# Two mix-out blocks woven together, retention rows scaled by two heads, x by token on another queue

## The chip, the cores and the metric

The kernel runs on one core of one Trainium2 chip. The metric is the device time of one execution in microseconds (us); a lower time is better. The core has a matrix engine (TensorE, PE in the profile, with its weight loads as PEld), a vector engine (VectorE, DVE), an engine for activations and scaled copies (ScalarE, ACT), GpSimd (POOL) and SyncE (SP), whose main work here is to request transfers.

## The reference

One layer of a hybrid decoder in float32, for 256 tokens of width 2048, all weights read once from memory:

```python
hn = rmsnorm(h, norm_mix_w)
q, k, v, g_ret, xr, yr, g_a, g_b = split(hn @ w_in)
ret = head_groupnorm(chunkwise_retention(rotary(q), rotary(k) * dk**-0.5, v), ret_gn_w)
ret_out = silu(g_ret) * ret                       # 8 heads, 256 values wide
rnn_out = gelu(yr) * rg_lru(causal_dwconv(xr))
merged = sigmoid(g_a) * (ret_out @ w_proj_ret) + sigmoid(g_b) * (rnn_out @ w_proj_rnn)
h = h + merged @ w_mix_out
h = h + memory_cross_attention(rmsnorm(h), rmsnorm(mem))    # 256 memory tokens
h = h + conv_gated_ffn(rmsnorm(h))                          # 5632 wide
return rmsnorm(h, final_norm_w)
```

## The kernel before, in words

**Weights in chunks.** Every matrix product is cut into blocks of 512 output columns, and the 2048 (or more) rows of weights of a block into chunks of four times 128 rows, 1 MB each. `weight_plan` lists the blocks in order, `weight_stream` flattens them to a list of chunks; the host lays the weights out in that order, so that each chunk is one transfer. The order of the list must be the order in which the products ask for chunks. Two places of the list are woven already: the first two blocks chunk by chunk, and three of the last ones, where the last chunk of each block comes after the others.

**High and low parts.** The products keep float32's precision: a chunk lands in a tile `raw` (three buffers), ScalarE casts it to a rounded high part `hi` (L267 for the first chunk on VectorE, L269 after), VectorE subtracts to get the low part `lo` (L270), half a chunk at a time (six buffers of each). TensorE makes three products for each pair of tiles, with high and low parts of the other operand (`s`), all by `mm` at L206. In a product by tokens (`steps_n`) the 24 matmuls of a chunk run over two tiles of tokens, four row tiles and three part products. `prefetch` requests a chunk (L244) and emits its casts; it keeps two chunks ahead of the one in use.

**Steps.** `chunks` is the loop under every product: it hands out a chunk, and at each chunk's end it runs what is due. `later(n, fn)` puts `fn` off by n + 1 chunk ends. A product is a generator (`steps_n`) that `ended` runs to its end, one chunk a step.

**Turning rows.** `by_dma(rows, then, wait)` turns a block of rows by token into columns by feature: two plane copies on ScalarE (`pl`, L380, with raised priority), two transposing transfers requested by SyncE (`pt`, L382), and, `wait` + 1 chunk ends later, two copies that join the planes (`f`, L391) and a call of `then`. For merged rows `then` is `turn_merged`, which splits them in high and low parts (`split_pair`, L420 to L424); for the residual stream it is `turn` with `split_cols` (L446, L447).

**Retention heads.** The heads are done in two groups of four. A head's rows go to `rc` (L632) with their mean and variance; after the fourth head `normalise` (L644 to L653) subtracts the mean and multiplies by the gate on VectorE for four heads and two tiles of tokens, and scales each by its reciprocal deviation on ScalarE into `rows` (L653, eight instructions), then calls `by_dma` for two blocks of rows with waits 2 and 3. In the second group, the rows of the recurrent branch are already coming through the same engines: their convolution is `conv_x` (L763 on ScalarE, L765 on VectorE).

**Merge and mix-out.** `gated` makes a block of one branch's projection times its gate; four blocks `mb` of the recurrent branch, then four `m` of the retention branch, added (L820) and turned. `residual` then makes the four blocks of merged times `w_mix_out`: each block needs all four merged blocks as its other operand, one of them in each of its four chunks. After a block it adds it to the residual row block (`nat`, L835), takes squares (L850, tile `junk`) and turns it. `memory_steps` (called ahead of each block) makes at the second block the eight sums of squares of the memory's rows on ScalarE (L488) and their deviation, and at the fourth loads the memory by feature.

**Order and queues.** The program is written in program order; a scheduler orders each engine's instructions by priority and by what they depend on, and each engine then works in that fixed order. Transfers are requested on SyncE's queue; only the four blocks of x by token (tiles `nat`, `load_x`, L223) are requested by ScalarE, after the casts of the fifth to eighth chunk. Constants (`cid`, `pa`, `pb`) follow the eighth chunk's weights, `pf` the twelfth's (L250 to L254). The sums of squares of x by token (L488) are emitted with the ninth and tenth chunk.

Of the kernel before, what the change touches and what calls it, by code (L numbers as in the profile page):

```python
# [17 lines left out]
P = 128  # L18
D = 2048
S = 256  # L20
NT = D // P
HEADS = 8
DK = 128
DV = 256
# [4 lines left out]
BW = 512  # L29
KC = 4  # L30
# [76 lines left out]
    return [(sum(sizes[:j]), n) for j, n in enumerate(sizes)]  # L107


def weight_stream():  # L110

    out = [
        [(w, row + k * P, n, c) for k, n in pieces(i, nk)]
        for i, (w, row, nk, c) in enumerate(weight_plan())
    ]
    out[:2] = [[one for pair in zip(*out[:2]) for one in pair]]
    out[-4:-1] = [[c for o in out[-4:-1] for c in o[:-1]] + [o[-1] for o in out[-4:-1]]]
    return [one for chunks in out for one in chunks]


# [10 lines left out]
def hybrid_layer(  # L131
# [16 lines left out]
    act, dve, pe, pool, sp = nc.scalar, nc.vector, nc.tensor, nc.gpsimd, nc.sync  # L148
# [15 lines left out]
    def big(shape, dt=F32, s="b"):  # L164
        return bp.tile(shape, dt, tag="big", name=nm(s))
# [52 lines left out]
    def load_x(n):  # L218
        while len(xin) < n:
            t = big([P, 2, BW], s="nat")  # L220
            rows = x[0].rearrange("(t p) d -> p t d", p=P)
            c = len(xin) * BW
            act.dma_start(out=t, in_=rows[:, :, c : c + BW])  # L223
            xin.append(t)

    at = [0]
# [1 line left out]
    def prefetch(n):  # L228
        while len(ahead) < n and taken[0] < len(stream):
            i = taken[0]  # L230
            name, row, nk, c = stream[i]
            taken[0] += 1
            size = nk * P * BW
            src = wall[at[0] : at[0] + size].rearrange("(p k n) -> p k n", p=P, k=nk)
            at[0] += size
            raw = wp.tile([P, KC, BW], F32, tag="raw", bufs=RAW_BUFS, name=nm("raw"))
            k2 = row // (KH * P)
            early = i < 2 * len(EARLY)
            own = early and i % 2 == 0
            cuts = range(nk + 1) if i < 2 else range(0, nk + 1, KH) if i < 6 else (0, nk)  # L240
            if own:
                xs.load(k2 + 1)
            for a, b in zip(cuts, cuts[1:]):
                sp.dma_start(out=raw[:, a:b, :], in_=src[:, a:b, :])  # L244
                if i == 0 and a == 0:
                    sp.dma_start(out=xs.rest[0], in_=xs.rest[1])
                elif own and a == 0:
                    xs.load(k2 + nk // KH)
            if i == 7:
                sp.dma_start(out=cid, in_=consts[:, 0:C_DEC])  # L250
                sp.dma_start(out=pa[:, 16:P], in_=by_feature[:, 16:P])
                sp.dma_start(out=pb, in_=by_feature[:, P : P + 80])
            if i == 11:
                sp.dma_start(out=pf.rearrange("p a n -> p (a n)"), in_=by_feature[:, P + 80 :])  # L254
            if i in (8, 9):
                for b in (2 * i - 16, 2 * i - 15):
                    sum_squares(xin[b], ss0, b, pin=True)
            parts = []
            for k in range(0, nk, KH):
                if own:  # L260
                    xs[k2 + k // KH]
                hi = wp.tile([P, KH, BW], F32R, tag="hi", bufs=PART_BUFS, name=nm("hi"))
                lo = wp.tile([P, KH, BW], F32R, tag="lo", bufs=PART_BUFS, name=nm("lo"))
                for cs in (slice(k, k + 1), slice(k + 1, k + 2)) if i < 2 else (slice(k, k + KH),):
                    ds = slice(cs.start - k, cs.stop - k)
                    if i == 0:
                        dve.tensor_copy(hi[:, ds], raw[:, cs, :])  # L267
                    else:
                        act.copy(hi[:, ds], raw[:, cs, :])  # L269
                    dve.tensor_tensor(  # L270
                        out=lo[:, ds], in0=raw[:, cs, :], in1=hi[:, ds].bitcast(F32), op=ALU.subtract
                    )
                parts.append((hi, lo))
            ahead.append(((row, c), parts))
            if i >= 4:
                load_x(min(4, i - 3))

    pending, step = [], [0]

    def later(n, fn):  # L280

        pending.append((step[0] + n + 1, fn))
# [18 lines left out]
    def ended(steps):  # L301

        for a in steps:
            pass
        return a
# [54 lines left out]
    def gemm_n(*args):  # L360
        return ended(steps_n(*args))
# [130 lines left out]
    def sums():  # L492
        return sp_.tile([P, 2, 4], F32, tag="ss0", name=nm("ss"))
# [103 lines left out]
    ret, words = [], []  # L597
# [5 lines left out]
    def retain(g, qr, kr, vs, dec, gates):  # L603

        stats = sp_.tile([P, 8, 2], F32, tag="mv", name=nm("mv"))
        raws = []

        def scores(hh):
            sc = small((P, 384))
            k, q = kr[hh // 2], qr[hh // 2]  # L610
            product(sc[:, 0:S], halves(k, hh % 2, slice(0, P)), halves(q, hh % 2), True, True)
            late = slice(P, S)
            product(sc[:, S : S + P], halves(k, hh % 2, late), halves(q, hh % 2, late), True, True)
            pr_ = tp.tile([P, 384], F32, tag="pret", bufs=2, name=nm("pret"))
            dve.tensor_tensor(out=pr_[:, 0:S], in0=sc[:, 0:S], in1=dec[:, hh, :], op=ALU.mult)
            dve.tensor_tensor(out=pr_[:, S:384], in0=sc[:, S:384], in1=dec[:, hh, 0:P], op=ALU.mult)
            phi, plo = (tp.tile([P, 384], F32R, tag="tmp", name=nm("ps")) for _ in range(2))
            act.copy(phi, pr_)
            dve.tensor_tensor(out=plo, in0=pr_, in1=phi.bitcast(F32), op=ALU.subtract)
            later(0, lambda: values(hh, phi, plo))  # L620

        def values(hh, phi, plo):
            vc = slice((hh % 2) * DV, (hh % 2 + 1) * DV)
            v0, v1 = ([t[:, tt, vc] for t in vs[hh // 2]] for tt in range(2))
            p0, p1, p2 = ([t[:, c * P : (c + 1) * P] for t in (phi, plo)] for c in range(3))
            ro = small()
            product(ro[:, 0, :], p0, v0, True, True)
            product(ro[:, 1, :], p1, v0, True, False)
            product(ro[:, 1, :], p2, v1, False, True)
            bn = sp_.tile([P, 2, 6], F32, tag="bn", name=nm("bn"))  # L630
            rc = tmp("rc")
            act.copy(rc, ro)  # L632
            for tt in range(2):
                dve.bn_stats(out=bn[:, tt, :], in_=rc[:, tt, :])
                dve.bn_aggr(out=stats[:, 2 * hh + tt, :], in_=bn[:, tt, :])
            raws.append(rc)
            if hh == 3:
                normalise()

        def normalise():  # L640
            rows = [big([P, 2, BW], s="rows") for _ in range(2)]
            rstd = rsqrt_small(stats[:, :, 1], 8, 1.0, GN_EPS).rearrange("p (h t) -> p h t", t=2)
            for tt in range(2):
                dve.tensor_scalar_mul(rstd[:, :, tt], rstd[:, :, tt], rs0[:, tt : tt + 1])  # L644
            for hh in range(4):
                for tt in range(2):
                    y = raws[hh][:, tt, :]
                    dve.scalar_tensor_tensor(
                        out=y, in0=y, scalar=stats[:, 2 * hh + tt, 0:1],
                        in1=gates[hh // 2][:, tt, (hh % 2) * DV : (hh % 2 + 1) * DV],  # L650
                        op0=ALU.subtract, op1=ALU.mult,
                    )
                    act.mul(rows[hh // 2][:, tt, (hh % 2) * DV : (hh % 2 + 1) * DV], y, rstd[:, hh, tt : tt + 1])  # L653
            for i, r in enumerate(rows):
                by_dma(r, words.append, 2 + i)

        for hh in range(4):
            later(hh, lambda hh=hh: scores(hh))

    for g in range(2):  # L660
        dec = big([P, 4, S], s="dec")
        vs, turned = [], ([], [])
        for b, o in enumerate((O_Q, O_K)):
# [6 lines left out]
            if b == 1:  # L670
                sp.dma_start(
                    out=dec,
                    in_=consts[:, C_DEC + g * 4 * S : C_DEC + (g + 1) * 4 * S].rearrange("p (h s) -> p h s", s=S),
# [144 lines left out]
    for b in range(4):  # L818
        m = gated(O_GA, "w_proj_ret", ret, b, big([P, 2, BW], s="m"))
        dve.tensor_add(m, m, mb[b])  # L820
        by_dma(m, turn_merged)


    hrow = [load_rows(x, c) for c in range(4)]
# [3 lines left out]
    def residual(w, st, out, wcol, steps=None):  # L828

        ss = sums()  # L830
        for b in range(4):
            if steps:
                steps(b)
            h = hrow[b]
            dve.tensor_add(h, h, gemm_n(w, 0, st, NT, b * BW))  # L835
            squares(h, ss, b)
            by_dma(hrow[b], lambda f, b=b: turn(f, b, out, wcol))
        return ss
# [261 lines left out]
```

## Time and profile before

| | us |
|---|---|
| median of 3 runs | 2025.03 |
| the other two | 2021.9, 2025.69 |
| profiled execution, whole time | 2022.28 |
| its span | 2020.5 |
| TensorE busy in it | 2002.3 |
| VectorE busy | 1264.3 |
| ScalarE busy | 1246.0 |

The span is the time from the first to the last recorded instruction of the profiled execution; its whole time is 1.8 us longer. TensorE is busy for 99% of it, at a mean granted clock of 0.996 of full speed. In lines of the profile, `L206` is the helper of all matmuls, `a<-b,c` is output and inputs by tile names, and `[1.98 <-DVE lo L270]` says how long an engine stood idle ahead of the instruction and what ended that.

### The profile page before, as it was taken

How to read it: one execution, taken by the hardware profiler on the slowest of the kernel's cores; microseconds unless marked ns; L12 is line 12 of the kernel's file. 1: busy time of each engine (PE TensorE's matmuls, PEld its weight loads, DVE VectorE, ACT ScalarE, POOL GpSimd, SP SyncE). 2: the span in 40 equal slices, each digit the busy share in tenths (PEclk: the TensorE clock that was granted, in tenths of full speed). 3: DMA queues.
4: the chain of work that ended last, by engine and by line, in shares of the span. 5: the costliest groups of instructions: out<-in, count | busy, mean ns of one | idle time of the engine just before them, and what ended most of it. 6: DMA issues, size and time to landing. Idle time of an engine off the chain costs nothing.

```text
span 2020.5 us, 23630 instructions
## 1 busy us (share of the span) xinstructions
PE 2002.3 (99%) x9060; PEld 1666.2 (82%) x9060; DVE 1264.3 (63%) x1563; ACT 1246.0 (62%) x1502; POOL 7.7 (0%) x12
## 2 busy tenths in 40 slices
PE   9999999999999999999999999999999999999998
PEld 7888888888888888788888888888888888888887
DVE  5856756888645555456555554567675577664675
ACT  6546547989434555478666556666774566644763
POOL 0000000000000000000000000000000000000000
PEclk9999999999999999999999999999999999999999
DMA  8665656665555566777766546667666566655663
GB/s 304 225 210 173 234 199 192 228 213 188 208 188 190 197 204 214 259 225 242 219 198 204 182 167 208 209 189 218 228 203 232 193 195 214 227 215 198 210 228 125
DMA packets 185153, 421.99 MB, mean 209 GB/s; under 512 B 127440, under 2 KB 132176, under 8 KB 139984
## 3 DMA queue, kind: packets, MB, share of 16 engines
q1 hardware_dynamic: 183520, 417.85, 62.2%
q10 hardware_dynamic: 1520, 2.63, 0.4%
q8 instruction: 71, 1.16, 0.2%
q14 instruction: 42, 0.34, 0.1%
HBM read 388.46 MB, written 2.10 MB: 193 GB/s over the span
## 4 chain that ended last, share of the span: by engine, by line
PE 97%; ACT 1%; DVE 1%; DMA 1%; issue 1%; SPq 0%; POOL 0%; POOLq 0%; DVEq 0%; ACTq 0%
PE acc L206 94%; PE sm L206 3%; DMA raw<-in_wall 1%; DVE lo L270 0%; ACT f L391 0%; DVE xr L765 0%; ACT pl L380 0%; ACT rows L653 0%; ACT hi L269 0%; POOL ro L507 0%; PE sm L209 0%; SPq L244 0%; DVE s L447 0%; ACT nat L1034 0%; DVE rows L404 0%
## 5 line engine op out<-in xcount | busy, mean ns | idle before, releaser
L206 PE MATMUL acc<-hi,s 128*128 128x512 f32 (+1 forms) x5680 | 1741.6, 388 | 4.2 <-ACT s L423 4.0
L270 DVE TENSOR_TENSOR lo<-raw,hi 128x1024 fp32r<-128x1024 f32 (+1 forms) x714 | 861.1, 1220 | 662.4 <-ACT hi L269 636.5
L206 PEld LDWEIGHTS acc<-hi,s 128*128 128x128 f32 x5680 | 1062.5, 188 | 222.1 <-ACT s L423 4.5
L206 PE MATMUL acc<-lo,s 128*128 128x512 f32 (+1 forms) x2840 | 1100.8, 388 | 2.0 <-DVE lo L270 2.0
L269 ACT CAST hi<-raw 128x1024 fp32r<-128x1024 f32 (+1 forms) x712 | 736.0, 1051 | 535.4 <-PE acc L206 466.7
L206 PEld LDWEIGHTS acc<-lo,s 128*128 128x128 f32 x2840 | 533.7, 188 | 111.6 <-DVE lo L270 2.7
L391 ACT COPY f<-pt 128x1024 uint16<-128x1024 uint16 x114 | 146.5, 1350 | 68.8 <-DMA pt<-pl 68.6
L380 ACT COPY pl<-rows 128x1024 uint16<-128x1024 uint16 x90 | 89.8, 1046 | 66.1 <-DVE rows L404 58.2
L404 DVE TENSOR_SCALAR rows<-acc,ro 128x512 f32<-128x512 f32 x68 | 47.8, 747 | 2.4 <-PE acc L206 2.4
L957 DVE SCALAR_TENSOR_TENSOR fv<-f,pf,fv 128x255 f32<-128x255 f32 (+1 forms) x88 | 35.8, 479 | 0.7 <-ACT fv L955 0.7
L957 DVE SCALAR_TENSOR_TENSOR fg<-f,pf,fg 128x255 f32<-128x255 f32 (+1 forms) x88 | 35.6, 478 | 0.0
L955 ACT ACTIVATE fv<-f,pf 128x256 f32<-128x256 f32 x44 | 22.9, 596 | 0.0
L955 ACT ACTIVATE fg<-f,pf 128x256 f32<-128x256 f32 x44 | 22.9, 594 | 0.0
L423 ACT ACTIVATE s<-fo 128x512 fp32r<-128x512 f32 x22 | 13.6, 635 | 14.1 <-DVE fo L977 14.1
L380 ACT COPY pl<-nat 128x1024 uint16<-128x1024 uint16 x16 | 16.0, 1046 | 9.6 <-DVE nat L835 9.6
L765 DVE SCALAR_TENSOR_TENSOR xr<-f,pa,xr 128x255 f32<-128x255 f32 (+2 forms) x48 | 20.1, 481 | 2.1 <-ACT xr L763 2.0
L446 ACT ACTIVATE s<-f,pb 128x256 fp32r<-128x256 f32 x48 | 20.4, 501 | 0.0
L447 DVE SCALAR_TENSOR_TENSOR s<-f,pb,s 128x256 fp32r<-128x256 f32 x48 | 19.9, 480 | 0.0
L206 PEld LDWEIGHTS sm<-s,s 128*128 128x128 f32 x144 | 18.8, 191 | 0.9
L206 PE MATMUL acc<-s,hi 128*128 128x512 f32 x64 | 17.6, 413 | 1.0 <-DVE hi L267 1.0
L206 PE MATMUL sm<-s,s 128*128 128x256 f32 (+1 forms) x144 | 18.6, 279 | 0.0
L421 DVE TENSOR_TENSOR s<-f,s 128x512 fp32r<-128x512 f32 x16 | 10.3, 687 | 10.0 <-ACT s L420 10.0
(154 smaller groups left out, 630.0 us busy)
## 6 DMA issues: line engine op xcount, KB each, us to landing
raw<-in_wall SPq DMA_DIRECT2D x352, 1024.0 KB, 4.9
raw<-in_wall SPq DMA_DIRECT2D x6, 512.0 KB, 6.4
nat<-in_x ACTq DMA_DIRECT2D x4, 512.0 KB, 8.2
nat<-in_x SPq DMA_DIRECT2D x4, 512.0 KB, 5.7
nat<-in_mem SPq DMA_DIRECT2D x4, 512.0 KB, 9.0
xt<-in_mem_t SPq DMA_DIRECT2D x8, 256.0 KB, 3.7
pt<-pl SPq DMA_TRANSPOSE x114, 4.9
xt<-in_x_t SPq DMA_DIRECT2D x7, 256.0 KB, 6.3
```

What stands on the lines that cost most here:

```text
L206: tc.keep_in_program_order(pe.matmul(*a, **k))
L269: act.copy(hi[:, ds], raw[:, cs, :])
L270: dve.tensor_tensor(out=lo[:, ds], in0=raw[:, cs, :], in1=hi[:, ds].bitcast(F32), op=ALU.subtract)
L380: act.copy(planes[:, :, h, :], words[:, h])
L391: act.copy(halves_[:, h], turned_[:, h])
L404: dve.tensor_scalar_mul(rows[:, tt, :], a[:, tt, :], r[:, tt : tt + 1])
L423: act.mul(t[:, :, 0:S], src, scale)
L446: act.activation(t[:, j, 0:S], src[:, j, :], AF.Identity, scale=wcol(j))
L447: dve.scalar_tensor_tensor(out=t[:, j, S:BW], in0=src[:, j, :], scalar=wcol(j), in1=t[:, j, 0:S].bitcast(F32), op0=ALU.mult, op1=ALU.subtract,
L765: dve.scalar_tensor_tensor(out=y[:, s:S], in0=z[:, 0 : S - s], scalar=p_cw(3 - s, t), in1=y[:, s:S], op0=ALU.mult, op1=ALU.add,)
L955: act.activation(y, z[:, j, :], AF.Identity, scale=pf[:, 2, t : t + 1], bias=pf[:, 3, t : t + 1])
L957: dve.scalar_tensor_tensor(out=y[:, s:S], in0=z[:, j, 0 : S - s], scalar=pf[:, 2 - s, t : t + 1], in1=y[:, s:S], op0=ALU.mult, op1=ALU.add,)
```

## The change

Three places change. (1) `weight_stream` and `residual`: the first two blocks of mix-out run in turn, three chunks of the first, three of the second, then the fourth of the first and the fourth of the second (`in_turn`, which the last blocks use already in its written-out form). The last merged block is turned with a wait of 3 instead of 1. Blocks three and four stay as they were. (2) `normalise`: the scaling of rows is split into `two_heads(0)` and `two_heads(1)`, each put off by `later` to one of the next two chunk ends, each turned with a wait of 4. (3) `load_x`: x by token is requested by SyncE behind the weights of the sixth to ninth chunk; `cid`, `pa`, `pb` move behind the ninth chunk's weights, `pf` behind the fourteenth's. The number of matmuls, casts and transfers stays the same.

```diff
@@ -107,6 +107,11 @@
     return [(sum(sizes[:j]), n) for j, n in enumerate(sizes)]
 
 
+def in_turn(products):
+
+    return [c for o in products for c in o[:-1]] + [o[-1] for o in products]
+
+
 def weight_stream():
 
     out = [
@@ -114,7 +119,9 @@
         for i, (w, row, nk, c) in enumerate(weight_plan())
     ]
     out[:2] = [[one for pair in zip(*out[:2]) for one in pair]]
-    out[-4:-1] = [[c for o in out[-4:-1] for c in o[:-1]] + [o[-1] for o in out[-4:-1]]]
+    out[-4:-1] = [in_turn(out[-4:-1])]
+    mix = [c[0][0] for c in out].index("w_mix_out")
+    out[mix : mix + 2] = [in_turn(out[mix : mix + 2])]
     return [one for chunks in out for one in chunks]
 
 
@@ -220,7 +227,7 @@
             t = big([P, 2, BW], s="nat")
             rows = x[0].rearrange("(t p) d -> p t d", p=P)
             c = len(xin) * BW
-            act.dma_start(out=t, in_=rows[:, :, c : c + BW])
+            sp.dma_start(out=t, in_=rows[:, :, c : c + BW])
             xin.append(t)
 
     at = [0]
@@ -246,11 +253,13 @@
                     sp.dma_start(out=xs.rest[0], in_=xs.rest[1])
                 elif own and a == 0:
                     xs.load(k2 + nk // KH)
-            if i == 7:
+            if i >= 5:
+                load_x(min(4, i - 4))
+            if i == 8:
                 sp.dma_start(out=cid, in_=consts[:, 0:C_DEC])
                 sp.dma_start(out=pa[:, 16:P], in_=by_feature[:, 16:P])
                 sp.dma_start(out=pb, in_=by_feature[:, P : P + 80])
-            if i == 11:
+            if i == 13:
                 sp.dma_start(out=pf.rearrange("p a n -> p (a n)"), in_=by_feature[:, P + 80 :])
             if i in (8, 9):
                 for b in (2 * i - 16, 2 * i - 15):
@@ -272,8 +281,6 @@
                     )
                 parts.append((hi, lo))
             ahead.append(((row, c), parts))
-            if i >= 4:
-                load_x(min(4, i - 3))
 
     pending, step = [], [0]
 
@@ -638,7 +645,6 @@
                 normalise()
 
         def normalise():
-            rows = [big([P, 2, BW], s="rows") for _ in range(2)]
             rstd = rsqrt_small(stats[:, :, 1], 8, 1.0, GN_EPS).rearrange("p (h t) -> p h t", t=2)
             for tt in range(2):
                 dve.tensor_scalar_mul(rstd[:, :, tt], rstd[:, :, tt], rs0[:, tt : tt + 1])
@@ -650,9 +656,17 @@
                         in1=gates[hh // 2][:, tt, (hh % 2) * DV : (hh % 2 + 1) * DV],
                         op0=ALU.subtract, op1=ALU.mult,
                     )
-                    act.mul(rows[hh // 2][:, tt, (hh % 2) * DV : (hh % 2 + 1) * DV], y, rstd[:, hh, tt : tt + 1])
-            for i, r in enumerate(rows):
-                by_dma(r, words.append, 2 + i)
+
+            def two_heads(i):
+                rows = big([P, 2, BW], s="rows")
+                for hh in (2 * i, 2 * i + 1):
+                    for tt in range(2):
+                        c = (hh % 2) * DV
+                        act.mul(rows[:, tt, c : c + DV], raws[hh][:, tt, :], rstd[:, hh, tt : tt + 1])
+                by_dma(rows, words.append, 4)
+
+            for i in range(2):
+                later(i, lambda i=i: two_heads(i))
 
         for hh in range(4):
             later(hh, lambda hh=hh: scores(hh))
@@ -818,7 +832,7 @@
     for b in range(4):
         m = gated(O_GA, "w_proj_ret", ret, b, big([P, 2, BW], s="m"))
         dve.tensor_add(m, m, mb[b])
-        by_dma(m, turn_merged)
+        by_dma(m, turn_merged, 1 if b < 3 else 3)
 
 
     hrow = [load_rows(x, c) for c in range(4)]
@@ -828,11 +842,16 @@
     def residual(w, st, out, wcol, steps=None):
 
         ss = sums()
+        products = [steps_n(w, 0, st, NT, b * BW) for b in range(4)]
         for b in range(4):
             if steps:
                 steps(b)
+                if b == 0:
+                    for one in products[:2]:
+                        for _ in range(NT // KC - 1):
+                            next(one)
             h = hrow[b]
-            dve.tensor_add(h, h, gemm_n(w, 0, st, NT, b * BW))
+            dve.tensor_add(h, h, ended(products[b]))
             squares(h, ss, b)
             by_dma(hrow[b], lambda f, b=b: turn(f, b, out, wcol))
         return ss
```

## The prediction

> **What bounds the kernel now.** I read the page's busy shares and chain first, then what TensorE (PE) waited for, then the timeline around each long wait, and the granted clock in stretches around them.
>
> ```profile
> span 2020.5 us, 23630 instructions
> ...
> PE 2002.3 (99%) x9060; PEld 1666.2 (82%) x9060; DVE 1264.3 (63%) x1563; ACT 1246.0 (62%) x1502; POOL 7.7 (0%) x12
> ...
> PE 97%; ACT 1%; DVE 1%; DMA 1%; issue 1%; SPq 0%; POOL 0%; POOLq 0%; DVEq 0%; ACTq 0%
> ```
>
> ```profile
> PE acc L206 <- ACT s L423: 4.0, 1, 4.0
> PE acc L206 <- DVE lo L270: 3.9, 5, 2.0
> ```
>
> PE is the bound: the chain that ended last runs on it for 97%. The change adds and removes no matmul, so it can act in two ways only: by the time in which PE stands still, and by the clock that PE is granted. The second view (waited for, total us, times, longest) says how little there is to gain: one wait of 4.0 us on a split (s, L423), and five on a low part of weights (lo, L270) that make 3.9, the longest 2.0. The timeline of PE tells where they stand (start, duration, and in brackets the idle time before and its releaser), and the windows give the clock (the number ahead of DMA share and GB/s is the mean granted clock).
>
> ```profile
> 20.51 2.45 PE L206 MATMUL acc<-s,lo 128*128 128x256 f32 x14 [1.42 <-DVE lo L270]
> ...
> 337.71 0.61 PE L206 MATMUL acc<-hi,s 128*128 128x512 f32 x2
> 340.31 0.50 PE L206 MATMUL acc<-lo,s 128*128 128x512 f32 x1 [1.98 <-DVE lo L270]
> ...
> 841.92 0.39 PE L206 MATMUL acc<-lo,s 128*128 128x512 f32 x1
> 846.35 1.52 PE L206 MATMUL acc<-hi,s 128*128 128x512 f32 x2 [4.04 <-ACT s L423]
> ...
> 851.33 0.40 PE L206 MATMUL acc<-lo,s 128*128 128x512 f32 x1
> 854.33 0.62 PE L206 MATMUL acc<-hi,s 128*128 128x512 f32 x2
> ...
> 859.77 0.62 PE L206 MATMUL acc<-hi,s 128*128 128x512 f32 x2
> ```
>
> ```profile
> 16.00:30.00 14.00, 12.38 (x54) 10.06 (x55) 9.44 (x14) 8.74 (x12) 0.00 (x0) 0.88 1.03 395
> 338.00:345.00 7.00, 5.02 (x23) 3.94 (x22) 5.16 (x7) 7.00 (x8) 0.00 (x0) 1.00 0.67 149
> 838.00:852.00 14.00, 9.96 (x34) 7.42 (x33) 4.79 (x5) 5.67 (x6) 0.00 (x0) 0.76 1.02 379
> ```
>
> Undisturbed, a chunk of 24 matmuls takes 859.77 - 854.33 = 5.44 us, 0.227 us each. The three stalls have three prices. The clock seems to fall to half, so 0.88 over 14 us is 2 x 0.12 x 14 = 3.4 us at half clock after the stall at 20.51; 0.76 over 14 us is 6.7 us at half clock after the stall at 846.35, twice as long; and after the stall at 340.31 there is none (1.00). A stretch of 3.4 us at half clock, if PE is busy in it, costs 1.7 us.
>
> **Second retention group's normalise (337.71).** PE would have gone on at 337.71 + 2 x 0.227 = 338.17; it went on at 340.31: 2.1 us lost, without half clock.
>
> ```profile
> 319.42 2.12 ACT L653 ACTIVATE rows<-rc,ro 128x256 f32<-128x256 f32 x5 [4.07 <-DVE ro L644]
> 321.44 1.98 ACT L380 COPY pl<-rows 128x1024 uint16<-128x1024 uint16 x2
> 323.33 1.31 ACT L653 ACTIVATE rows<-rc,ro 128x256 f32<-128x256 f32 x3
> ...
> 325.49 1.99 ACT L380 COPY pl<-rows 128x1024 uint16<-128x1024 uint16 x2
> ```
>
> ```profile
> 339.02 3.50 DVE L270 TENSOR_TENSOR lo<-raw,hi 128x1024 fp32r<-128x1024 f32 x3
> ```
>
> Before, ScalarE (ACT) makes all eight scalings of rows and four plane copies in one go: 2.12 + 1.98 + 1.31 + 1.99 = 7.4 us. Behind them on ACT stand the copies f (L391) and the convolution's first products (L763), behind those on VectorE (DVE) the rest of the convolution (L765), and behind that the late lo, which starts at 339.02 and takes 3.50 / 3 = 1.17 us, so is ready at about 340.2. After, two heads are scaled one chunk end after the other, as pieces that step aside for other work: the order of ACT puts the two f, a hi cast and the convolution's four products ahead of the first scalings. All of the 7.4 us leaves the path to that lo (ready near 332.8, 5.3 us before 338.17), or, if the f copies have to wait for their transposes and only one half leaves it, 3.7 us (ready at 336.5, still 1.7 us early). Either way the stall goes: -2.1 us. The scalings that move behind then run beside matmuls; the next to be late would be the retention words, which are used only by the projection of the retention. In the first group the same move meets no stall of its own; I cost it at nothing, covered by that same room of some 5 us, and if the cover were gone by a row like the 1.98 us above.
>
> **First two mix-out blocks in turn (846.35).** The fourth chunk of block 0 needs the fourth merged block, whose rows are only just made. PE should have started it at 841.92 + 0.227 = 842.15.
>
> ```profile
> 843.12 2.51 ACT L391 COPY f<-pt 128x1024 uint16<-128x1024 uint16 x2
> 845.67 1.15 ACT L423 ACTIVATE s<-f 128x512 fp32r<-128x512 f32 x2
> ```
>
> The stall is 846.35 - 842.15 = 4.20 us, and the 11 matmuls from 846.35 to 851.33 take 4.98 us instead of 11 x 0.227 = 2.49. Together 6.7 us. After, three chunks of block 1 stand between: the fourth merged block is wanted at 842.15 + 3 x 5.44 = 858.47, while the splits above end near 846.8. Even with its turn put two chunk ends later than the others' there are several us of room. -6.7 us.
>
> What is late next? Blocks 0 and 1 now end one chunk apart, at 858.47 + 5.44 = 863.91 and at 869.35, instead of four, and what follows each (residual, squares, planes, transposes, split by columns) falls together, with the eight squares of the memory's rows between, all on ACT. In the order of after, ACT does between the hi cast of block 2's second chunk and that of its third, without a hi cast between: two planes of block 0, its two squares, eight squares of memory, two f, three column splits and two planes of block 1, the fourth split and block 1's two squares. Their durations, from where the same operations stand in before:
>
> ```profile
> 856.40 2.00 ACT L380 COPY pl<-nat 128x1024 uint16<-128x1024 uint16 x2 [1.04 <-DVE nat L835]
> 858.30 0.63 ACT L850 ACTIVATE junk<-nat 128x512 f32<-128x512 f32 x1
> ...
> 859.54 0.62 ACT L488 ACTIVATE junk<-nat 128x512 f32<-128x512 f32 x1
> ...
> 864.46 1.99 ACT L269 CAST hi<-raw 128x1024 fp32r<-128x1024 f32 x2
> 866.35 2.56 ACT L391 COPY f<-pt 128x1024 uint16<-128x1024 uint16 x2
> ...
> 869.72 1.71 ACT L446 ACTIVATE s<-f,pb 128x256 fp32r<-128x256 f32 x4
> 871.33 2.94 ACT L269 CAST hi<-raw 128x1024 fp32r<-128x1024 f32 x3
> ```
>
> ```profile
> 858.42 4.51 SPq L382 DMA_TRANSPOSE pt<-pl  x2
> ```
>
> ```profile
> DMA to landing us min/median/max: 3.1/4.9/7.3
> ```
>
> Planes 858.30 - 856.40 = 1.90; a pair of squares 859.54 - 858.30 = 1.24; the eight squares 864.46 - 859.54 = 4.92; f 2.56; four splits 871.33 - 869.72 = 1.61. Block 0's planes started 2.07 us after its end (856.40 against 854.33), so here at 863.91 + 2.07 = 865.98. Then 1.90 + 1.24 + 4.92 brings ACT to 874.04. The transposes are issued 2.0 us after the planes' start (858.42 against 856.40), at 868.0 and, as one follows another, about 1.3 later, and land by the median of 4.9 us at 872.9 and 874.2: just in time for the f, so 2.56 + 1.24 + 1.61 + 1.90 = 7.31 us more, to 881.35. With the longest landing, 7.3 us, the second f starts some 1.3 us later; with the shortest nothing is gained, as ACT is busy till then. Then the hi cast (half of 1.99, 1.0 us) ends at 882.35, and the lo, 1.17 us, at 883.5.
>
> PE wants this third chunk of block 2 at 869.35 + 2 x 5.44 = 880.23: it waits 2.1 us for hi, does two matmuls (0.45), and waits 0.7 for lo. A new stall of 2.8 us, which the trace of before doesn't show; its bounds are 0 (the scheduler's order leaves a gap that I don't see, or the squares run shorter) and 4.1 (slowest landing). I take 2.8. All following hi casts are in a row then, 1 us each against a chunk's 5.44 us for two, so there is no third stall; SyncE's (SP) next weights behind block 1's transposes are for block 3's second chunk, wanted three chunks after 883, at about 899.
>
> Is it followed by half clock? The row at 20.51 had 1.42 us of idle time (and 3.4 us at half clock after it), that at 340.31 had 1.98 (and none), that at 846.35 4.04 (and 6.7 us). 2.8 us lies between; I take one stretch, +1.7 us, bounds 0 and 3.4. The Trainium skill, "TensorE: Matmul & The Clock Gate", Part 1, says that the clock is halved after at least one idle window of about 3.4 us and that the windows run freely; by that rule alone a stall of 2.8 us would never halve it. The row at 20.51, with 1.42 us idle, doesn't agree, and the length of 3.4 us does.
>
> **x by token on SP's queue.** Before, the four blocks of x by token are requested by ACT after the casts of the fifth to eighth chunk; after, by SP right behind the weights of the sixth to ninth, with constants moved behind (cid, pa, pb from the eighth to the ninth chunk, pf from the twelfth to the fourteenth).
>
> ```profile
> 26.36 5.53 SPq L525 DMA_DIRECT2D xt<-in_x_t  x2
> ```
>
> ```profile
> 44.39 3.89 ACT L269 CAST hi<-raw 128x1024 fp32r<-128x1024 f32 x4
> 48.19 0.57 ACT L412 COPY c<-acc 128x512 f32<-128x512 f32 x1
> ```
>
> ```profile
> 46.17 4.62 DVE L270 TENSOR_TENSOR lo<-raw,hi 128x1024 fp32r<-128x1024 f32 x4
> ```
>
> ```profile
> 49.87 0.71 PE L206 MATMUL acc<-hi,s 128*128 128x512 f32 x2
> ```
>
> It takes four requests off ACT and puts them into SP's queue, where the weights behind them wait only for the time to issue. SP stands 5.53 us at 26.36 in before, and the ninth chunk's weights wait behind it; moved requests shorten that. The stall at 20.51 is older than any of this and stays. One thing gets tighter: in ACT's order the copy c of the first half of q (L412) now stands ahead of the tenth chunk's casts, not behind. It waits for PE's half at about 46.7, and so that chunk's first lo moves from 46.17 + 1.17 = 47.3 to about 49.5, with PE wanting it after two matmuls from 49.87. Still in time, by under 1 us. I cost the whole part at 0, bounds -1 (SP's wait) and +1.5 (the tenth chunk late by a row such as 1.42).
>
> **The sum.** -2.1 - 6.7 + 2.8 + 1.7 + 0 = -4.3 us. The profiled execution took 2022.28 us (span 2020.5 and 1.8 around it), so it would be 2018.0. The median of the three runs, 2025.03, lies 2.75 above. Part of that may be half clock after the stall at 340.31, which the profile happened not to have and which goes with the stall (0 to 1.7). Against the median the gain is thus 4.3 to 6.0; I take the middle, 5.2, and forecast 2019.8 us. A measurement of this kernel can tell about 0.2%, 4 us, from no change, so the forecast is near that line.
>
> **Rivals.**
> *No new stall in block 2.* Then -2.1 - 6.7 = -8.8: 2013.5 by the profiled execution's time, 2016.2 from the median. For it: the 2.8 us are what is left of some 15 us of ACT's work added up, so a fifth off the terms takes them away. Against: the order of ACT is fixed, and nothing in the list is optional. 0.2.
> *New stall, but no half clock*, since it is split by two matmuls, as after 340.31: -6.0, 2016.3 or 2019.0. For it the 1.00 of that stretch, against it the 0.88 of 16 to 30. 0.25.
> *Slower: block 0's transposes land late.* They are issued in the middle of 1 MB weight transfers, and ACT, being in order, holds block 2's hi cast behind the f that waits for them. Up to a landing of 6 us (the second, issued at 869.3, is then there as the first f ends at 875.3) it costs nothing, beyond that each us is a us of stall. With two stretches of half clock (3.4) a landing of 9 us makes 2.8 + 3.0 + 3.4 - 8.8 = +0.4, and one of 13 us +4.4, 2029.4. It decides from 8.6 us on. No transpose of before took over 7.3, so 0.07.
> *The stalls only move*: a weight or a split late somewhere in the reordered stretches (the tenth chunk, the fourth chunk of block 0, the second group's words) pays back most, -1 to -3: 2022 to 2024. 0.13.
> The forecast has the rest, 0.35.
>
> **How the numbers follow.** Low is the first rival with the profiled execution's time, 2013.5. High takes in the fourth rival, 2024.8. Outside lie the slow rival and the tails, under 2 in 10. Faster by over 0.2% means below 2021.0: all of the first rival, 0.23 of the second and half of the forecast's own (its middle is 1.2 us inside, its unknown terms are of 1.5 us and more), 0.2 + 0.23 + 0.17 = 0.6. Slower by over 0.2%, above 2029: the slow rival and the part of unknown costs on top of the fourth, 0.1. Within: 0.3.
>
> **What would show it.** Right: no wait of PE on s (L423's successor) in the first mix-out blocks, no wait on lo of about 2 us at 338, a wait on hi and then on lo in the middle of block 2, some 54 us after the mix-out begins, and a clock below 1.00 in the stretch after it. Wrong: PE running through block 2 without a wait (ACT then shows the hi cast before 880); a new wait with raw as its cause near 50 us; f waiting for pt over 1 us before block 2's third chunk; or a time above 2025 with these waits gone.

## The result, and the profile after

The changed kernel takes 2018.46 us (median of 11 runs, 2015.83 to 2021.29); the kernel before, in the same comparison, 2022.92 (11 runs, 2021.44 to 2025.69). The ratio is 0.9977, with a 95% interval of 0.9968 to 0.9985: 4.5 us less, clear of noise, though only 0.2%. The profiled execution took 2018.6 us, its span 2016.8.

The page's head and chain, as they were shown of before:

```profile
span 2016.8 us, 23617 instructions
...
PE 2001.7 (99%) x9060; PEld 1665.9 (83%) x9060; DVE 1263.6 (63%) x1563; ACT 1241.8 (62%) x1502; POOL 7.7 (0%) x12
...
PE 96%; DMA 1%; DVE 1%; ACT 1%; issue 1%; SPq 0%; POOLq 0%; POOL 0%; DVEq 0%; ACTq 0%
```

PE's waits (total us, times, longest), its timeline around the longest of them, and the stretches with the granted clock:

```profile
PE acc L213 <- DVE lo L279: 3.2, 6, 1.4
PE acc L213 <- ACT hi L278: 2.3, 1, 2.3
```

```profile
20.70 2.34 PE L213 MATMUL acc<-s,lo 128*128 128x256 f32 x14 [1.42 <-DVE lo L279]
...
877.92 0.39 PE L213 MATMUL acc<-lo,s 128*128 128x512 f32 x1
880.56 0.73 PE L213 MATMUL acc<-hi,s 128*128 128x512 f32 x2 [2.26 <-ACT hi L278]
881.82 0.54 PE L213 MATMUL acc<-lo,s 128*128 128x512 f32 x1 [0.53 <-DVE lo L279]
...
885.81 0.62 PE L213 MATMUL acc<-hi,s 128*128 128x512 f32 x2
```

```profile
16.00:30.00 14.00, 11.93 (x53) 9.61 (x52) 9.92 (x13) 8.81 (x12) 0.00 (x0) 0.88 1.03 408
338.00:345.00 7.00, 7.00 (x33) 5.88 (x32) 4.81 (x4) 6.81 (x11) 0.00 (x0) 1.00 1.08 255
838.00:852.00 14.00, 14.00 (x63) 11.60 (x62) 3.74 (x4) 6.06 (x7) 0.00 (x0) 1.00 1.03 393
880.00:890.00 10.00, 8.91 (x31) 6.89 (x32) 7.88 (x10) 10.00 (x13) 0.00 (x0) 0.83 0.80 256
```

Both waits that were to go are gone: from 338 to 345 and from 838 to 852 PE is busy for the whole stretch, at full clock. A new one stands in the third chunk of mix-out's block 2 (blocks counted from 0), on hi and then on lo, with 2 x 0.17 x 10 = 3.4 us at half clock behind it.

Where the time came from is read off three marks, small products that both traces have: one near 50 us, the first `sm<-xr,rgw` behind the stall at 338, and the first `sm<-s,s` of the memory's attention. First before, then after (the counts at the ends of some rows differ because the views cut the rows; the starts are those of the same matmuls):

```profile
49.51 0.60 PE L206 MATMUL sm<-diag,ones 128*128 128x128 f32 x4
...
344.07 1.24 PE L206 MATMUL sm<-xr,rgw 128*128 128x256 f32 x5
...
985.30 1.96 PE L206 MATMUL sm<-s,s 128*128 128x256 f32 x15
```

```profile
49.70 0.49 PE L213 MATMUL sm<-diag,ones 128*128 128x128 f32 x3
...
341.99 1.89 PE L213 MATMUL sm<-xr,rgw 128*128 128x256 f32 x8
...
981.03 3.04 PE L213 MATMUL sm<-s,s 128*128 128x256 f32 x24
```

The distance is +0.19 us at the first, -2.08 at the second and -4.27 at the third: -2.27 between the first two (the normalise part), -2.19 between the last two (mix-out; some 0.4 of it is a delay at 930.49 us of the profile before, in the product behind mix-out, that the execution after did not have). The spans differ by 3.7, so later stages took about 0.6 more.

### The profile page after: what moved, and what is told of

It reads as the page before. It is cut to its first block, busy times and chain, and to the rows that moved or that the text cites. A ratio compares the mean times of both kernels' runs of the same rounds, so it can differ in the third digit from the quotient of the medians.

```text
span 2016.8 us, 23617 instructions
## 1 busy us (share of the span) xinstructions
PE 2001.7 (99%) x9060; PEld 1665.9 (83%) x9060; DVE 1263.6 (63%) x1563; ACT 1241.8 (62%) x1502; POOL 7.7 (0%) x12
## 4 chain that ended last, share of the span: by engine, by line
PE 96%; DMA 1%; DVE 1%; ACT 1%; issue 1%; SPq 0%; POOLq 0%; POOL 0%; DVEq 0%; ACTq 0%
PE acc L213 93%; PE sm L213 3%; DMA raw<-in_wall 1%; DMA pt<-pl 0%; DVE lo L279 0%; ACT hi L278 0%; ACT pl L387 0%; ACT f L398 0%; DVE fv L976 0%; DVE fg L976 0%; PE sm L216 0%; ACT s L453 0%; SPq L251 0%; ACT junk L869 0%; DVE rows L411 0%
## 5 line engine op out<-in xcount | busy, mean ns | idle before, releaser
L430 ACT ACTIVATE s<-fo 128x512 fp32r<-128x512 f32 x22 | 13.6, 633 | 14.2 <-DVE fo L996 14.2
L428 DVE TENSOR_TENSOR s<-f,s 128x512 fp32r<-128x512 f32 x16 | 10.3, 685 | 9.8 <-ACT s L427 9.8
```

The lines of the kernel that those rows point to most:

```text
L430: act.mul(t[:, :, 0:S], src, scale)
```

## The experiments

In order of the questions: do the parts add, and what is the new stall made of? "The last two marks" are those of the section above, read in each run's own profile.

**Mix-out part alone** (on the kernel before).

```diff
-        by_dma(m, turn_merged)
+        by_dma(m, turn_merged, 1 if b < 3 else 3)
...
+    out[mix : mix + 2] = [in_turn(out[mix : mix + 2])]
```

> The kernel before with the mix-out part alone. Theory (the three parts add; the mix-out part trades a stall of 4.2 us and 2.5 of half clock for one of 2.8 and some 2.0 of half clock): about -1.8 against before, some 2021; the wait at 340 is still there (about 2 us on lo), and block 2 of mix-out shows the wait on hi of about 2.3 and on lo of 0.5. Rival (the mix-out part brings most of the 4.5, the normalise part is hidden): -3 to -4.5.

Measured: 2020.62 us against 2022.08, ratio 0.9992 (0.9983 to 1.0001). The wait at 338 is there, and so is the new stall:

```profile
338.47 0.50 PE L213 MATMUL acc<-lo,s 128*128 128x512 f32 x1 [1.94 <-DVE lo L277]
...
881.06 0.73 PE L213 MATMUL acc<-hi,s 128*128 128x512 f32 x2 [2.49 <-ACT hi L276]
882.32 0.50 PE L213 MATMUL acc<-lo,s 128*128 128x512 f32 x1 [0.53 <-DVE lo L277]
```

Between the last two marks this profile takes 639.28 us, 1.95 less than before (641.23), and between the first two 294.54, as before (294.56). So of the 6.7 us that the old stall and its half clock cost, weaving the blocks gains some 1.5 to 2: it turns one stall into a shorter one, later. The trace speaks against the rival (most of the gain from here); the times alone don't rule it out, as the ratio's interval reaches from -3.4 to +0.2 us.

**Normalise part alone.**

```diff
-            for i, r in enumerate(rows):
-                by_dma(r, words.append, 2 + i)
...
+            for i in range(2):
+                later(i, lambda i=i: two_heads(i))
```

> The kernel before with the normalise part alone. Theory: the wait on lo at 340 is gone, -2.1 to -2.3 us, some 2020.7; the wait of 4 us on s with half clock in mix-out stays. Rival (another instruction is late at 338 when the scalings leave): 0 to -1.

Measured: 2020.26 us against 2022.08, ratio 0.9989 (0.9980 to 0.9998), 1.8 (by the medians) to 2.2 us (by the ratio) less, as expected, though the interval reaches from -4.0 to -0.4. Between the first two marks this profile takes 292.28 us, 2.28 less than before, where the whole change shows 2.27. PE runs through the stretch from 337 to 346, and the stall of mix-out is as before:

```profile
337.00:346.00 9.00, 9.00 (x42) 7.53 (x41) 6.17 (x8) 8.64 (x14) 0.00 (x0) 1.00 1.09 256
```

```profile
843.23 1.52 PE L206 MATMUL acc<-hi,s 128*128 128x512 f32 x2 [4.04 <-ACT s L423]
```

**x by token on SyncE alone.**

```diff
-            act.dma_start(out=t, in_=rows[:, :, c : c + BW])
+            sp.dma_start(out=t, in_=rows[:, :, c : c + BW])
...
```

The rest of the edit moves these requests and those of the constants behind the chunks named in the change.

> The kernel before with x by token on SyncE's queue alone. Theory: 0, within 1 us; the stall at 20.5 stays. Rival (the tenth chunk is late, as the copy of q's first half stands ahead of its casts): +1.5 to +3, with a wait on lo near 50 us.

Measured: 2023.45 us against 2022.08, ratio 1.0007 (0.9998 to 1.0016). No wait stands near 50 us, so the tenth chunk is in time and that rival falls. What this profile shows beside the profile of before is another thing: the same stall at 338 was followed by half clock here, where before had none.

```profile
338.66 0.50 PE L206 MATMUL acc<-lo,s 128*128 128x512 f32 x1 [1.94 <-DVE lo L272]
```

```profile
337.00:346.00 9.00, 7.34 (x25) 5.97 (x26) 6.24 (x7) 7.50 (x10) 0.00 (x0) 0.81 0.72 184
```

2 x 0.19 x 9 = 3.4 us at half clock, which cost 1.58 us: 296.14 between the first two marks against 294.56. Whether the 1.4 us of the medians are this chance or the part itself, this run alone doesn't tell.

Do the parts add? In the traces they do: -2.28 and -1.95 alone, -2.27 and -2.19 together. The medians can't tell: -1.5, -1.8 and +1.4 make -1.9, where the whole change made -4.5, and each of the four has some 1.8 us of uncertainty to either side.

**Changed kernel without the x part.**

```diff
-            sp.dma_start(out=t, in_=rows[:, :, c : c + BW])
+            act.dma_start(out=t, in_=rows[:, :, c : c + BW])
...
-            if i >= 5:
-                load_x(min(4, i - 4))
...
+            if i >= 4:
+                load_x(min(4, i - 3))
```

The constants go back to their old places with it.

> The changed kernel without its third part: x by token is requested by ScalarE as before. Theory (that part is worth nothing): 2018 to 2018.5, as the changed kernel. Rival (it costs what it showed alone, 1.4 us): 2016.9; second rival (the sum of the parts run alone, -1.6 and -2.2, holds): 2018.6 less x's share, 2018.3, and x's part is what the whole owes nothing to.

Measured: 2017.97 us (7 runs), ratio to before 0.9973 (0.9963 to 0.9984), against 0.9977 (0.9968 to 0.9985) with it: the same within the intervals. The new stall is there (2.52 and 0.53 us):

```profile
879.08 0.73 PE L213 MATMUL acc<-hi,s 128*128 128x512 f32 x2 [2.52 <-ACT hi L276]
880.34 0.80 PE L213 MATMUL acc<-lo,s 128*128 128x512 f32 x1 [0.53 <-DVE lo L277]
```

**Squares of the memory's rows spread out**, the test of the new stall. In the changed kernel:

```diff
-        if b == 1:
+        if b == 2:
             ss = sums()
             for c in range(4):
-                sum_squares(mnat[c], ss, c)
-            rsms.append(rstd_rows(ss))
+                later(c, lambda c=c: sum_squares(mnat[c], ss, c))
+            later(4, lambda: rsms.append(rstd_rows(ss)))
```

> The changed kernel, but the squares of the memory's rows are made two at a time at the four chunk ends after the third mix-out block has begun, not all eight ahead of the second. Theory (the new stall is the sum of ScalarE's work between two hi casts): ScalarE's eight squares, 4.9 us, leave the way, so both waits in block 2 go, with their half clock: -4.9 against the changed kernel, about 2013.6 (before: -9). Rival (block 2's hi cast is held by the transposes or by the weights' landing): a wait of 2 to 3 us stays, 2018.

Measured: 2014.09 us (5 runs, 2011.68 to 2016.41), ratio to before 0.9957 (0.9945 to 0.9970). ScalarE makes two squares at a time, and the casts pass between them; PE has no wait and full clock where it stood before:

```profile
874.00:892.00 18.00, 18.00 (x82) 14.89 (x80) 12.04 (x16) 18.00 (x33) 0.00 (x0) 1.00 0.64 206
```

So the stall was ScalarE's work standing in one lump ahead of the cast, not the landing of transposes or weights. Between the last two marks this profile takes 634.08 us, 4.96 less than the changed kernel's (639.04): that is what the lump cost. The medians say 4.4 (2018.46 - 2014.09, from two comparisons) and the ratios to before 4.0.

**Four squares made twice.** The opposite dose, in the changed kernel:

```diff
-            for c in range(4):
+            for c in (0, 1, 0, 1, 2, 3):
```

> The changed kernel with four of the eight squares of the memory's rows made twice (same values, same place): 2.46 us more of ScalarE's work ahead of block 2's third hi cast. Theory (the new stall is the sum of ScalarE's work): the wait on hi grows from 2.26 by 2.2 to 2.5 us (the 0.28 us that the copy f waited for its transposes goes first) to 4.5 to 4.7, the wait on lo stays 0.5, and half clock lasts twice as long, 6.8 us: +2.3 and +1.7, 2022 to 2022.5. Rival (hi waits for something else, the transposes or the weights): the wait stays 2.3, 2018.5.

Measured: 2020.76 us (11 runs), 2.3 more than the changed kernel; ratio to before 0.9988 (0.9979 to 0.9997). The two ratios' intervals overlap, but the trace shows the same: 641.32 us between the last two marks, 2.28 more than the changed kernel's.

```profile
881.18 1.22 PE L213 MATMUL acc<-hi,s 128*128 128x512 f32 x2 [4.32 <-ACT hi L278]
882.44 0.80 PE L213 MATMUL acc<-lo,s 128*128 128x512 f32 x1
```

```profile
876.00:881.00 5.00, 0.86 (x4) 0.38 (x2) 1.77 (x4) 5.00 (x10) 0.00 (x0) 0.86 0.13 25
881.00:888.00 7.00, 6.78 (x18) 4.96 (x19) 5.27 (x5) 7.00 (x9) 0.00 (x0) 0.61 0.76 224
```

The wait on hi grew by 4.32 - 2.26 = 2.06 us for 2.46 us of ScalarE's work (expected 2.2 to 2.5), the wait on lo went (expected to stay), and half clock lasted 2 x 0.14 x 5 + 2 x 0.39 x 7 = 6.9 us, twice as long. The mechanism holds; the median came out 1.2 us under the range given. The wait on lo of 0.5 us is missing from it: the two matmuls ahead of it took 1.26 us at half clock (881.18 to 882.44), as long as the two matmuls and the wait together in the changed kernel (880.56 to 881.82). And of the half clock 1.4 us lie in the stall itself, where they cost nothing: only the 5.5 us behind it do, some 2.7, or 1.0 more than the 1.7 of the changed kernel, where 1.7 more was expected. In sum 2.1 more on hi, 0.8 less on lo and 1.0 more of half clock make the 2.3.

**Squares spread, without the x part.** The spread squares and ScalarE's requests of x as before:

> The spread squares of the memory's rows without the third part of the change. Theory (x by token worth nothing): as with it, 2014.1, within 1 us. Rival (x by token on SyncE costs 1.4 us): 2012.7.

Measured: 2012.92 us (5 runs), ratio to before 0.9944 (0.9930 to 0.9958), against 0.9957 (0.9945 to 0.9970) with the x part. In all three pairs the kernel with x on SyncE has the higher ratio to before (by 1.4, 0.8 and 2.6 us), but each pair lies within its intervals, and no wait of the traces goes with it. Nor does time: of the profiles that had no half clock near 20 us, the four with it take 47.90 to 48.25 us up to the first mark, the four without it 47.71 to 48.95; between the first two marks the changed kernel takes 292.29 us with and without it, and between the last two the spread one 634.08 with and 634.07 without it. In two of the five profiles without it, the last two, the ninth chunk is late by some tenths, here by 0.48 us:

```profile
43.52 0.98 PE L213 MATMUL acc<-s,lo 128*128 128x256 f32 x6 [0.48 <-DVE lo L277]
```

None of the five with it shows that wait, which fits the argument that the x part shortens it. Its net effect is not settled: the traces show none, the three pairs lean to a small cost.

**Squares spread from the first block on**, `b == 0` in place of `b == 2`, where ScalarE has several idle us.

> As the spread squares, but two at a time from the chunk ends after the first mix-out block has begun, where ScalarE stands idle for several us. Theory: no wait in block 2 either, 2014, unless the squares wait for the memory's rows to land and hold the casts behind them. Rival (rows land too late, a wait in blocks 0 or 1): a wait of 1 to 3 us on hi near 850, 2016 to 2018.

Measured: 2013.67 us (5 runs), ratio to before 0.9949 (0.9937 to 0.9962). The squares did wait 2.66 us for the memory's rows, but nothing late came of it there: PE is undisturbed from 838 to 852. This profile has a wait of 1.28 us on a split (s) at 922.00, in the product behind mix-out; the normalise part alone has one of 0.71 at that place, and whether the early squares make it longer is not tested.

```profile
842.35 0.63 ACT L495 ACTIVATE junk<-nat 128x512 f32<-128x512 f32 x1 [2.66 <-DMA nat<-in_mem]
```

The three spread versions beat both kernels, by 8.7, 11.3 and 10.3 us against before (by their ratios), and can't be told from one another.

## Why the prediction was right

**Forecast and size.** 2019.8 was forecast, 2018.46 measured, in a range of 2013.5 to 2024.8. The sum for the profiled execution was -4.3; the spans differ by -3.7 and the medians by -4.5. Some of this is luck: both profiled executions had half clock behind the stall near 20 us (0.88 in both), which only two of the ten profiles had. Had one of them been without, the spans would differ by some 1 to 2 us more or less (an estimate: up to the first mark these two take 49.51 and 49.70 us, the eight others 47.71 to 48.95).

**Normalise.** Forecast -2.1, read -2.27 between the marks. The late lo was to be ready near 332.8; this is the row of it after (the last one shown), with what stands ahead of it on ScalarE and VectorE:

```profile
318.03 2.57 ACT L398 COPY f<-pt 128x1024 uint16<-128x1024 uint16 x2 [2.49 <-DMA pt<-pl]
...
321.41 2.08 ACT L777 ACTIVATE xr<-f,pa 128x256 f32<-128x256 f32 x4
323.39 1.69 ACT L665 ACTIVATE rows<-rc,ro 128x256 f32<-128x256 f32 x4
...
325.93 1.99 ACT L387 COPY pl<-rows 128x1024 uint16<-128x1024 uint16 x2
...
328.78 1.70 ACT L665 ACTIVATE rows<-rc,ro 128x256 f32<-128x256 f32 x4
330.39 1.03 ACT L278 CAST hi<-raw 128x1024 fp32r<-128x1024 f32 x1
```

```profile
324.65 2.84 DVE L779 SCALAR_TENSOR_TENSOR xr<-f,pa,xr 128x253 f32<-128x253 f32 x7
...
331.46 1.23 DVE L279 TENSOR_TENSOR lo<-raw,hi 128x1024 fp32r<-128x1024 f32 x1 [1.32 <-ACT hi L278]
```

It ends at 332.7. The reason held: the copies f and the convolution now stand ahead of the scalings, so VectorE is through with the convolution at 327.5 and the lo no longer queues behind it. But not all of the 7.4 us left the path, as the prediction had it: f waited 2.49 us for its transposes, and eight scalings and two planes, 1.69 + 1.99 + 1.70 = 5.4 us, still stand ahead of the hi cast at 330.39, for which this lo now waits. That 332.7 meets 332.8 so closely is luck; that over 5 us of room are left is not.

**Mix-out's old stall.** -6.7: from 838 to 852 PE is busy all the time.

**The new stall.** Its place, cause and size came out: the profile names 2.26 + 0.53 = 2.8 us of idle time, in the third chunk of block 2, first on hi, then on lo. The 2.8 worked out were counted as time lost, though, from the moment at which PE wanted each part, and counted so it is 3.2: 880.56 - 878.15 = 2.41 on hi (2.1 forecast; the third chunk was due at 877.92 + 0.227 = 878.15), and 881.82 - 880.56 less two matmuls of 0.227, 0.81, on lo (0.7 forecast). The rows of ScalarE after show the steps of the sum:

```profile
863.91 2.00 ACT L387 COPY pl<-nat 128x1024 uint16<-128x1024 uint16 x2 [1.06 <-DVE nat L854]
...
867.05 0.61 ACT L495 ACTIVATE junk<-nat 128x512 f32<-128x512 f32 x1
...
872.33 2.56 ACT L398 COPY f<-pt 128x1024 uint16<-128x1024 uint16 x2 [0.28 <-DMA pt<-pl]
...
876.57 1.98 ACT L387 COPY pl<-nat 128x1024 uint16<-128x1024 uint16 x2
...
879.48 3.87 ACT L278 CAST hi<-raw 128x1024 fp32r<-128x1024 f32 x4
```

Planes, squares, f, splits and planes take 879.48 - 863.91 = 15.57 us, where 865.98 to 881.35 was worked out, 15.37 (all some 2.1 us earlier than worked out, PE's third chunk too, as the stall at 338 is gone). The transposes were there 0.28 us after ScalarE was free for them: the landing was just in time, as worked out. The slower rival, which hung on a late landing, was not seen: in the four profiles with this lump the wait of f for pt there is 0 to 0.55 us, the longest without the x part, and the stall's wait on hi 2.52 us then instead of 2.26.

**Half clock behind it.** One stretch of 3.4 us, 1.7 us of loss, was forecast. Measured: from 878.15, where the third chunk was due, to the row at 885.81 lie 12 matmuls, 2.72 us at 0.227, so 4.94 us were lost; less the 2.41 on hi and the 0.81 on lo, that leaves 1.7, as forecast. The 4.94 are what spreading the squares won back between the marks (4.96).

**Against the median.** The step that failed is small: I took part of the distance between the profiled execution and the median of three runs as half clock that goes with the change, and forecast 5.2 against the median. That median of 2025.03 was itself high: further runs put before at 2022.9 in the first comparison and at 2022.1 and 2022.95 in the others. That half clock can follow the stall at 338 was shown (x by token alone), only not how often; the sum against the profiled execution's own time, -4.3, was the better forecast of the measured -4.5.

**x by token.** Forecast 0 between -1 and +1.5. The traces show no cost and the pairs of kernels lean to +0.8 to +2.6, none of them clear of noise, so the term is not settled. The copy c now stands ahead of the tenth chunk's casts, as foreseen, and PE had no wait there.

**The rivals.** No new stall: refuted by the rows. The stall without half clock: refuted in the three profiles that have that stall (after, mix-out part alone, without the x part), each with half clock. The slower one: not seen, as said above. Stalls that only move: true of mix-out for 4.9 of its 6.7 us, which the sum had as its own terms.

## What to carry to other kernels

When work is moved to clear one stall, add up what the engine that feeds the critical one will now do without a break, in its fixed order, and compare that lump with how far ahead its feeds are; here 15.6 us of ScalarE, and 1.0 us for the cast behind them, met a PE that wanted the cast's result 14.2 us after they began (863.91 to 878.15): a stall, and the addition gave its size. Then look which item of the lump is free to go elsewhere: the squares of the memory's rows could, and spreading them was worth about as much as the whole change. A stall's price is its length and the clock behind it, and the second varies from run to run, so the sum is best made against the profiled execution's own time.

## What the runs showed of the hardware

The clock did not follow the length of a stall alone. Over ten profiles, the stall near 20 us (1.09 to 1.80 us idle) had 3.4 us of half clock behind it in two and none in eight; that at 338 (1.94 to 1.98) in one of three; that in block 2 (2.26 to 2.52, and 0.53) in three of three, for one stretch of 3.4 us; stalls of 4.0 and 4.3 us in all four, for two stretches. Within such a stretch the granted clock is a half: from 882.5 to 885.5 of the profile after it is 0.50 in every half microsecond.

The Trainium skill, "TensorE: Matmul & The Clock Gate", Part 1, says that the clock is halved after at least one idle window of about 3.4 us, and that the window runs freely. The length of 3.4 us agrees; the condition of a whole idle window is contradicted by the row at 20.70, with 1.42 us idle ahead of it and 0.88 as the mean clock from 16 to 30. That a stall falls into one window at one time and is shared by two at another would fit the counts above, but no run here shows it.
